# Exchanging real and imaginary rows in an S5 scan: by ScalarE and a second matrix product, or by transfers

## The chip, the core and the metric

The kernel runs on one core of a Trainium2 chip. The metric is device time in microseconds (us), from the start of the program to its end. The core has TensorE (PE in the rows; its weight loads are PEld), VectorE (DVE), ScalarE (ACT), GpSimd (POOL) and SyncE (SP), each of which works through its own instructions in the order in which they are written, and 16 DMA engines that move data between HBM (the device memory) and SBUF (the on-chip memory). Matrix products land in PSUM. SPq and ACTq are the parts of SyncE and ScalarE that issue transfers: a transfer that has to wait there for its source or its buffer holds up all that is queued behind it on that engine.

## The reference, cut to what matters

One inference step of a two-layer decoder, 2048 prompt tokens and 8 sample tokens, width 1024. Each layer projects its normed input and runs four head groups of width 256 side by side; the third of them (C) is S5, a diagonal complex state space model with 16 channel groups of 64 complex states. All of it is float32.

```python
proj = jnp.einsum('btd,de->bte', hn, w_in)      # 15 column groups, among them s_u and s_g
...
# _s5: u (B, T, 256) -> y, last state; x0 is the state before
bu_re = jnp.einsum('gpc,btgc->btgp', bb_re, ug)
bu_im = jnp.einsum('gpc,btgc->btgp', bb_im, ug)
def combine(e1, e2):
    a1r, a1i, b1r, b1i = e1
    a2r, a2i, b2r, b2i = e2
    return (a2r * a1r - a2i * a1i, a2r * a1i + a2i * a1r,
            a2r * b1r - a2i * b1i + b2r, a2r * b1i + a2i * b1r + b2i)
_, _, xr, xi = lax.associative_scan(combine, (A_re, A_im, bu_re, bu_im), axis=1)
y = jnp.einsum('gcp,btgp->btgc', c_re, xr) - jnp.einsum('gcp,btgp->btgc', c_im, xi)
...
mix = jnp.concatenate([ret_out, ml_out, s5_out, xa_out], axis=-1)
y = x + jnp.einsum('bte,ed->btd', mix, w_out)
```

## The kernel before

Each layer works through its prompt in four units of 512 tokens, so there are eight units. A unit is a row of weight groups of 256 columns (`m_v`, `s_u`, four `out` groups of the unit before, then `m_k` and so on to `r_g`); `group` multiplies each with the normed input `hT` or the mixed output `mix`. A weight arrives as `wraw`, ScalarE makes its high part `whi`, and VectorE and GpSimd make the low parts `wlo` (L338); three products of high and low parts stand for one exact one. Between two pieces of a group, `step_sides` moves every head group's generator on by one `yield`. That gives the program's order; a scheduler then lays out each engine's instructions, so a yield more or less shifts how much of the other groups' work stands between two steps.

S5 is the generator `s_core`. Four time steps are folded into one column, so a unit has 128 columns. The first 64 partitions hold real parts and the other 64 imaginary parts. The projected input goes to HBM as `ud` and comes back as X. Four times per unit (a quarter: four channel groups) there is a product of X with `Wi` into PSUM; a rotation by a table (`Cs`, `Sn`) that turns the complex decay into a real one; four real scans; the rotation back; and a product with `TW` that gives the output. A rotation needs each value's partner, the imaginary part beside the real one, which lies 64 partitions away. `swap` (L1267) fetches it by two transfers from SBUF to SBUF, 64 rows each: once ahead of the scans, from `V` into `Vs`, once after them, from `y` into `ys`. The program's own names are missing there: `t` in the rows is `V`, `y` or `t1`, and `sv` is `Vs` or `ys`. `xs` holds the rotated state, `xprev` the state that is carried on. The tables come from `s5_pre`, a generator that is run once per layer and writes them to HBM; `s_tables` loads them for each quarter.

The lines that the prediction speaks of: L1278 clears `xprev` at the start of a layer, L1282 loads X, L1289 is the product with `Wi`, L1294 and L1305 are the swaps, L1297 and L1309 the products that wait for them, L1302 the scans, L1310 GpSimd's product, L1311 the subtraction into `xs`, L1312 the copy into `xprev`, L1321 the product with `xs`. In the rows all matrix products stand as L180, transposes as L184, ScalarE's work as L187 and transfers as L190 or L193, since helpers write them; the rows' tile names tell them apart.

## Time and profile before

| | us |
|---|---|
| median of 3 runs | 2450.93 |
| lowest and highest | 2448.82, 2454.46 |
| the profiled execution | 2451.49 |
| its span, first to last instruction | 2449.7 |

| engine | busy us | share |
|---|---|---|
| TensorE, matmuls | 2175.0 | 89% |
| TensorE, weight loads (beside them) | 1989.2 | 81% |
| VectorE | 1663.0 | 68% |
| ScalarE | 978.3 | 40% |
| GpSimd | 845.2 | 35% |

The mean granted TensorE clock is 0.946 of full speed. The profile is of one execution. A row such as `L1309 DVE ... sv<-sv,sCS` gives the source line, the engine, the operation and what it writes and reads. A wait is named by what ended it, on the left the one that waited. The chain that ended last is followed back from the last instruction: at each step to what released it.

### The profile page before, as it was taken

Reading aid. Unit: us, or ns where it says so; the run is one execution under the profiler, and the core shown is the slowest. Engines: PE = TensorE matmul, PEld = TensorE weight load, DVE = VectorE, ACT = ScalarE, POOL = GpSimd, SP = SyncE. Lnnn points to the kernel's source line nnn. Section 1 sums busy time; section 2 is a strip of 40 time slices with the busy share of each in tenths; the row PEclk is TensorE's granted clock in tenths of the full one; section 3 lists DMA queues with packets and bytes.
Section 4 is the critical chain, followed back from the end, with each engine's and each line's share of the span. In section 5 each row is a group of like instructions: output and inputs, shape, how many; then the busy total and the mean of one; then the engine's idle time right before and its main releaser. Section 6 shows DMA issues by size and latency. Waiting matters only on the chain.

```text
span 2449.7 us, 44181 instructions
## 1 busy us (share of the span) xinstructions
PE 2175.0 (89%) x16130; PEld 1989.2 (81%) x16130; DVE 1663.0 (68%) x4003; ACT 978.3 (40%) x2152; POOL 845.2 (35%) x755
## 2 busy tenths in 40 slices
PE   7899957897889989987889999878989899999898
PEld 6788856897788878875888889777989787888788
DVE  7987835646675789773874767347576678868474
ACT  4554423342433544243442454223443354433343
POOL 2443312232233435442322343213332244434243
PEclk9999988899999999998999999888999999999899
DMA  7525374447374435735435442784446643573522
GB/s 222 168 86 179 99 109 96 132 137 94 88 208 130 127 115 171 217 99 102 121 110 178 118 132 77 171 183 87 87 101 208 198 125 113 161 247 121 101 64 105
DMA packets 355529, 329.78 MB, mean 135 GB/s; under 512 B 109144, under 2 KB 310040, under 8 KB 355312
## 3 DMA queue, kind: packets, MB, share of 16 engines
q1 hardware_dynamic: 329472, 266.53, 43.2%
q10 hardware_dynamic: 25840, 60.43, 7.8%
q8 instruction: 127, 2.08, 0.4%
q14 instruction: 90, 0.74, 0.1%
HBM read 265.40 MB, written 45.73 MB: 127 GB/s over the span
## 4 chain that ended last, share of the span: by engine, by line
PE 34%; DVE 15%; DMA 14%; issue 3%; ACT 2%; SPq 2%; POOL 1%; ACTq 0%; DVEq 0%; POOLq 0%
PE pm L180 24%; PE ps L180 8%; DMA sv<-t 4%; DMA wraw<-w_in 3%; PE ps L184 2%; DVE wlo L338 2%; SPq L190 2%; DVE sm L207 1%; DVE t L1302 1%; DMA X<-ud 1%; DMA s5im_p<-xprev 1%; DVE sm L206 1%; DVE sm L208 1%; DMA ud<-U 1%; DVE sv L1297 1%
## 5 line engine op out<-in xcount | busy, mean ns | idle before, releaser
L338 POOL TENSOR_TENSOR wlo<-wraw,whi 128x512 fp32r<-128x512 f32 (+1 forms) x280 | 400.5, 1435 | 655.9 <-ACT whi L187 513.7
L180 PE MATMUL pm<-hT,whi 128*128 128x512 f32 (+1 forms) x2240 | 610.1, 361 | 5.3 <-ACT whi L187 5.3
L180 PE MATMUL pm<-whi,hT 128*128 128x256 f32 (+1 forms) x3072 | 593.4, 289 | 16.3 <-ACT whi L187 13.7
L180 PEld LDWEIGHTS pm<-whi,hT 128*128 128x128 f32 x3072 | 488.8, 193 | 23.1 <-ACT whi L187 14.3
L187 ACT ACTIVATE whi<-wraw 128x512 fp32r<-128x512 f32 (+1 forms) x560 | 342.2, 629 | 392.1 <-PE pm L180 250.2
L180 PE MATMUL pm<-wlo,hT 128*128 128x256 f32 (+1 forms) x1536 | 440.8, 288 | 28.3 <-DVE wlo L338 27.1
L180 PEld LDWEIGHTS pm<-hT,whi 128*128 128x128 f32 x2240 | 397.4, 194 | 64.5 <-ACT whi L187 5.7
L180 PE MATMUL pm<-hT,wlo 128*128 128x512 f32 (+1 forms) x1120 | 398.0, 359 | 25.7 <-DVE wlo L338 24.3
L180 PE MATMUL pm<-whi,mix 128*128 128x256 f32 x2048 | 382.1, 286 | 9.1 <-ACT whi L187 5.5
L338 DVE TENSOR_TENSOR wlo<-wraw,whi 128x512 fp32r<-128x512 f32 (+1 forms) x280 | 248.7, 891 | 153.2 <-ACT whi L187 130.7
L180 PEld LDWEIGHTS pm<-whi,mix 128*128 128x128 f32 x2048 | 324.3, 193 | 11.3 <-ACT whi L187 5.8
L180 PEld LDWEIGHTS pm<-wlo,hT 128*128 128x128 f32 x1536 | 295.7, 193 | 31.6 <-DVE wlo L338 28.9
L180 PE MATMUL pm<-wlo,mix 128*128 128x256 f32 x1024 | 292.7, 287 | 8.8 <-DVE wlo L338 8.8
L180 PEld LDWEIGHTS pm<-hT,wlo 128*128 128x128 f32 x1120 | 215.7, 193 | 59.4 <-DVE wlo L338 26.6
L180 PEld LDWEIGHTS pm<-wlo,mix 128*128 128x128 f32 x1024 | 197.5, 193 | 10.1 <-DVE wlo L338 9.8
L1310 POOL TENSOR_TENSOR t<-t,sCS 128x512 f32<-128x512 f32 x32 | 45.7, 1427 | 216.5 <-DVE t L1302 66.7
L187 ACT ACTIVATE Pt<-ps,sm 128x256 f32<-128x256 f32 x128 | 58.9, 472 | 129.6 <-DVE sm L951 123.4
L1297 DVE TENSOR_TENSOR sv<-sv,sCS 128x512 f32<-128x512 f32 x32 | 25.0, 782 | 99.6 <-DMA sv<-t 99.6
L959 POOL TENSOR_TENSOR Pt<-Pt,sm 128x512 f32<-128x512 f32 x32 | 46.3, 1448 | 56.3 <-DVE sm L957 40.7
L207 DVE SCALAR_TENSOR_TENSOR sm<-sm,sm 128x8 f32<-128x8 f32 (+4 forms) x210 | 60.5, 290 | 3.5
L1309 DVE TENSOR_TENSOR sv<-sv,sCS 128x512 f32<-128x512 f32 x32 | 26.8, 838 | 51.1 <-DMA sv<-t 51.0
L1398 DVE TENSOR_TENSOR xr<-xr,pm 128x512 f32<-128x512 f32 x56 | 37.9, 678 | 31.2 <-PE pm L180 23.1
(442 smaller groups left out, 3717.5 us busy)
## 6 DMA issues: line engine op xcount, KB each, us to landing
wraw<-w_in SPq DMA_DIRECT2D x416, 256.0 KB
wraw<-w_out SPq DMA_DIRECT2D x128, 256.0 KB
sCS<-CS SPq DMA_DIRECT2D x32, 512.0 KB
sv<-t SPq DMA_DIRECT2D x128, 128.0 KB
xd<-xr SPq DMA_DIRECT2D x56, 256.0 KB
...
```

The costliest lines, as they stand in the source:

```text
L180: self.nc.tensor.matmul(out, lhsT, rhs, start=start, stop=stop, skip_group_check=skip)
L184: self.nc.tensor.transpose(out, in_, self.ident[:K, :K])
L187: self.nc.scalar.activation(out, in_, f, **kw)
L190: self.nc.sync.dma_start(out, in_)
L206: v.tensor_tensor(t, y, y, OP.mult)
L207: v.scalar_tensor_tensor(t, t, -0.5, b, op0=OP.mult, op1=OP.mult)
L338: e.tensor_tensor(lo[q][:, :, :n], r[q][:, :, :n], h.bitcast(F32), OP.subtract)
L959: e.tensor_tensor(Pt[:, 2 * x:2 * x + 2], Pt[:, 2 * x:2 * x + 2], sm_[:, 2 * x:2 * x + 2, None].to_broadcast([128, 2, MEM]), OP.mult)
L1297: v.tensor_tensor(Vs, Vs, Sn, OP.mult)
L1309: v.tensor_tensor(ys, ys, Sn, OP.mult)
L1310: gp.tensor_tensor(t1, y, Cs, OP.mult)
L1398: v.tensor_tensor(xr, xr, ps.rearrange("p (t c) -> p t c", t=2), OP.add)
```

## The change

The partner rows are no longer fetched by transfers. Ahead of the scans, ScalarE copies the product out of PSUM into `B` with the halves exchanged (two instructions of 64 rows), and VectorE reads the same PSUM for the other part. After the scans the partner isn't fetched at all: GpSimd writes y times `Cs` into `A`, VectorE writes y times `Sn` into `B`, both with their rows in place, and the sum that was `xs` is left to TensorE: `A` is multiplied with the table as before, and `B` with a third table, in which the two halves of the rows are exchanged. `B` stands one column later than `A`, whose first column is `xprev`, so the product with `B` has 127 columns. The carried state needs one column of the exchanged `B`, which ScalarE copies into `sh` in two instructions of 64 rows, and VectorE adds it to `A`'s last column.

Beside that: `xprev` is taken anew in each layer from a pool of two buffers; `s_core` has two more yields between the load of X and its first use, a quarter three instead of five, and one more after `yT`; `s5_pre` fetches `Bst` and `ct` ahead of where they are used, with three more yields; `TW` has a third part, which `s_tables` loads too; the pool `t2p` has a twelfth buffer.

```diff
@@ -135,7 +135,7 @@
         self.cp = e(tc.tile_pool(name="cp", bufs=1))
         self.wp = e(tc.tile_pool(name="wp", bufs=2))
         self.g4p = e(tc.tile_pool(name="g4p", bufs=16))
-        self.t2p = e(tc.tile_pool(name="t2p", bufs=11))
+        self.t2p = e(tc.tile_pool(name="t2p", bufs=12))
         self.t1p = e(tc.tile_pool(name="t1p", bufs=3))
         self.s64p = e(tc.tile_pool(name="s64p", bufs=12))
         self.smp = e(tc.tile_pool(name="smp", bufs=17))
@@ -255,7 +255,6 @@
         for t in self.Sr + self.Cm:
             nc.vector.memset(t, 0.0)
         self.mprev = c("mprev", [4, 8])
-        self.xprev = c("xprev", [128, SG])
         self.hS = [c(f"hS{i}", [128, 8, 40], F32R) for i in range(2)]
         for i in range(2):
             nc.vector.tensor_copy(self.hS[i].rearrange("p a b -> p (a b)"), zero)
@@ -269,7 +268,7 @@
         self.memd = []
         for l in range(self.depth):
             self.stab.append(dict(
-                Wi=self.dram([128, SG, 128], f"Wi{l}"), TW=self.dram([128, 2, 1024], f"TW{l}"),
+                Wi=self.dram([128, SG, 128], f"Wi{l}"), TW=self.dram([128, 3, 1024], f"TW{l}"),
                 CS=self.dram([128, 2, SG, 128], f"CS{l}"), Kd=self.dram([32, 16, 112], f"Kd{l}"), ab=self.dram([128, 3, SG], f"ab{l}"),
                 C1=self.dram([128, SG, SC], f"C1{l}")))
             self.memd.append((self.dram([128, 2, MEM], f"mk{l}"), self.dram([128, 2, GW], f"mv{l}")))
@@ -1078,6 +1077,13 @@
             self.dma(ar[64 * h:64 * h + 64], I["s5_a_re"][l].rearrange("g p -> p g"))
             self.dma(ai[64 * h:64 * h + 64], I["s5_a_im"][l].rearrange("g p -> p g"))
         self.dma(dt, AP(I["s5_log_dt"][l], 0, [[0, 128], [1, SG]]))
+        Bst = P1([2, SG, SC], "Bst")
+        for h in range(2):
+            for w in range(2):
+                src = I["s5_b_re" if h == w else "s5_b_im"][l]
+                self.dma(Bst[64 * h:64 * h + 64, w], src.rearrange("g p c -> p g c"))
+        yield
+        yield
         self.pexp(dt, SG)
         mag, th, cs, sn, k, tmp, thl = S(), S(), S(), S(), S(), S(), S()
         v.tensor_tensor(mag, ar, dt, OP.mult)
@@ -1141,13 +1147,17 @@
         sgn = self.smc[:, 0:1]
         fis = S()
         v.tensor_scalar(fis, fi, sgn, None, op0=OP.mult)
-        yield
-
-        Bst = P1([2, SG, SC], "Bst")
-        for h in range(2):
+        cts = []
+        for gh in range(2):
+            ct = P1([2, 128], "ct")
             for w in range(2):
-                src = I["s5_b_re" if h == w else "s5_b_im"][l]
-                self.dma(Bst[64 * h:64 * h + 64, w], src.rearrange("g p c -> p g c"))
+                src = I["s5_c_re" if w == 0 else "s5_c_im"][l].rearrange("g c p -> (g c) p")
+                s_ = src[gh * 128:(gh + 1) * 128, :]
+                self.dma(ct[:, 0, 64 * w:64 * w + 64], s_)
+                self.dma(ct[:, 1, 64 * (1 - w):64 * (1 - w) + 64], s_)
+            cts.append(ct)
+        yield
+
         Bb = P1([2, SG, SC], "Bb")
         bt = P1([SG, SC], "bt")
         bc = lambda x: x[:, :, None].to_broadcast([128, SG, SC])
@@ -1161,13 +1171,9 @@
         v.tensor_scalar(pims, pw[:, 1], sgn, None, op0=OP.mult)
 
         C1, C2 = packC[:, 0], packC[:, 1]
+        yield
         for gh in range(2):
-            ct = P1([2, 128], "ct")
-            for w in range(2):
-                src = I["s5_c_re" if w == 0 else "s5_c_im"][l].rearrange("g c p -> (g c) p")
-                s_ = src[gh * 128:(gh + 1) * 128, :]
-                self.dma(ct[:, 0, 64 * w:64 * w + 64], s_)
-                self.dma(ct[:, 1, 64 * (1 - w):64 * (1 - w) + 64], s_)
+            ct = cts[gh]
             ps = self.bank()
             self.tr(ps[:, 0:128], ct[:, 0, :])
             self.tr(ps[:, 128:256], ct[:, 1, :])
@@ -1231,6 +1237,9 @@
             v.tensor_tensor(W5, W5, w5, OP.subtract)
             self.dma(tab["TW"][:, 1, 256 * q:256 * q + 256].rearrange("p (g c) -> p g c", g=4),
                      W5[:, :, 1:5, :].rearrange("p g s c -> p g (s c)"))
+            for h in range(2):
+                self.dma(tab["TW"][64 * h:64 * h + 64, 2, 256 * q:256 * q + 256].rearrange("p (g c) -> p g c", g=4),
+                         W5[64 - 64 * h:128 - 64 * h, :, 1:5, :].rearrange("p g s c -> p g (s c)"))
             yield
             yield
 
@@ -1257,17 +1266,13 @@
     def s_tables(self, l, q):
         tab = self.stab[l]
         gs = slice(4 * q, 4 * q + 4)
-        TW, Wi = self.tb([128, 2, 256], "sTW", bufs=2), self.tb([128, 4, 128], "sWi")
+        TW, Wi = self.tb([128, 3, 256], "sTW", bufs=2), self.tb([128, 4, 128], "sWi")
         CS = self.tb([128, 2, 4, 128], "sCS")
         self.dma(Wi, tab["Wi"][:, gs])
         self.dma(CS.rearrange("p a g j -> p a (g j)"), tab["CS"][:, :, gs].rearrange("p a g j -> p a (g j)"))
         self.dma(TW, tab["TW"][:, :, 256 * q:256 * q + 256])
         return TW, Wi, CS[:, 0], CS[:, 1]
 
-    def swap(self, out, in_):
-        self.dma(out[0:64], in_[64:128])
-        self.dma(out[64:128], in_[0:64])
-
     def s_core(self, u, l, b):
         nc, v, gp = self.nc, self.nc.vector, self.nc.gpsimd
         while not self.pre_done[l]:
@@ -1275,51 +1280,56 @@
         if b == 0:
             self.abt = self.cp.tile([128, 3, SG], F32, name=self.nm("ab"), tag="ab", bufs=1)
             self.dma(self.abt, self.stab[l]["ab"])
+            self.xprev = self.cp.tile([128, SG], F32, name=self.nm("xprev"), tag="xprev", bufs=2)
             v.memset(self.xprev, 0.0)
         tb = self.s_tables(l, 0)
         X = self.g4([128, 8, 128], n="X")
         for s in range(4):
             self.dmaa(X[32 * s:32 * s + 32], AP(u["ud"], s * 128, [[512, 32], [32 * 512, 8], [1, 128]]))
         yield
+        yield
+        yield
         Y = self.g4([128, 8, 128], n="Y")
         for q in range(4):
             TW, Wi, Cs, Sn = tb
+            gq = slice(4 * q, 4 * q + 4)
             ps = self.bank()
             for g in range(4):
                 self.mm(ps[:, g * 128:(g + 1) * 128], Wi[:, g], X[:, 2 * q + g // 2], True, True)
             p3 = ps.rearrange("p (g j) -> p g j", g=4)
-            V, Vs, t1 = self.t2([128, 4, 128]), self.tb([128, 4, 128], "sv", bufs=2), self.t2([128, 4, 128])
-            self.act(V, p3)
+
+            B, t1, A = self.t2([128, 4, 128], n="sB"), self.t2([128, 4, 128], n="sy"), self.t2([128, 4, 129], n="sA")
             v.tensor_tensor(t1, p3, Cs, OP.mult)
-            self.swap(Vs, V)
-            yield
-            yield
-            v.tensor_tensor(Vs, Vs, Sn, OP.mult)
-            v.tensor_tensor(t1, t1, Vs, OP.add)
-            y = V
+            for h in range(2):
+                self.act(B[64 * h:64 * h + 64], p3[64 - 64 * h:128 - 64 * h])
+            v.tensor_copy(A[:, :, 0], self.xprev[:, gq])
+            v.tensor_tensor(B, B, Sn, OP.mult)
+            v.tensor_tensor(t1, t1, B, OP.add)
             for g in range(4):
                 gg = 4 * q + g
-                v.tensor_tensor_scan(y[:, g], self.abt[:, 2, gg:gg + 1].to_broadcast([128, 128]), t1[:, g],
+                v.tensor_tensor_scan(t1[:, g], self.abt[:, 2, gg:gg + 1].to_broadcast([128, 128]), t1[:, g],
                                      self.xprev[:, gg:gg + 1], OP.mult, OP.add)
-            ys = Vs
-            self.swap(ys, y)
-            yield
-            xs = self.t2([128, 4, 129], n="xs")
-            v.tensor_copy(xs[:, :, 0], self.xprev[:, 4 * q:4 * q + 4])
-            v.tensor_tensor(ys, ys, Sn, OP.mult)
-            gp.tensor_tensor(t1, y, Cs, OP.mult)
-            v.tensor_tensor(xs[:, :, 1:129], t1, ys, OP.subtract)
-            v.tensor_copy(self.xprev[:, 4 * q:4 * q + 4], xs[:, :, 128])
+
+            gp.tensor_tensor(A[:, :, 1:129], t1, Cs, OP.mult)
+            v.tensor_tensor(B, t1, Sn, OP.mult)
+            yield
+            sh = self.sm([128, 16])[:, :4]
+            for h in range(2):
+                self.act(sh[64 * h:64 * h + 64], B[64 - 64 * h:128 - 64 * h, :, 127])
             if q < 3:
                 tb = self.s_tables(l, q + 1)
             yield
+            v.tensor_tensor(self.xprev[:, gq], A[:, :, 128], sh, OP.add)
             yield
             po = self.bank()
             for a in range(2):
                 self.mm(po[:, a * 128:(a + 1) * 128], TW[:, 0, a * 128:(a + 1) * 128], X[:, 2 * q + a], a == 0, False, True)
-            for g in range(4):
-                self.mm(po[64 * (g % 2):64 * (g % 2) + 64, (g // 2) * 128:(g // 2 + 1) * 128],
-                        TW[:, 1, g * 64:(g + 1) * 64], xs[:, g, 0:128], False, g == 3, True)
+            for a in range(2):
+                for w, x, c0 in ((1, A, 0), (2, B, 1)):
+                    for e in range(2):
+                        g = 2 * a + e
+                        self.mm(po[64 * e:64 * e + 64, a * 128 + c0:(a + 1) * 128], TW[:, w, g * 64:(g + 1) * 64],
+                                x[:, g, 0:128 - c0], False, w == 2 and g == 3, True)
             self.act(Y[:, 2 * q:2 * q + 2].rearrange("p a j -> p (a j)"), po[:, :256])
         yd = self.dram([2, 8, SC, 4, 128], "yd")
         for g2 in range(2):
@@ -1330,6 +1340,7 @@
         yT = self.g4([128, 2, UT], n="yT")
         for gh in range(2):
             self.dmaa(yT[:, gh], AP(yd, gh * 128 * 512, [[512, 128], [1, 512]]))
+        yield
         yield
         if b == self.NU - 1:
             for h, on in enumerate(("s5re_p", "s5im_p")):
```

Three places show what this makes of the engines' order. The first is VectorE in the first quarter of the second unit of layer 1, before; `wlo` are weight splits, `xr` the output groups' sums.

```order
L1293 TENSOR_TENSOR t_3167_17640<-ps_17633,sCS_17556 128x512
L1308 COPY xs_17852<-xprev 128x4
L1398 TENSOR_TENSOR xr_17645<-xr_17645,pm_17647 128x512
L338 TENSOR_TENSOR wlo_17768<-wraw_17706,whi_17767 128x2x256
L1297 TENSOR_TENSOR sv_17639<-sv_17639,sCS_17556 128x512
L1298 TENSOR_TENSOR t_3167_17640<-t_3167_17640,sv_17639 128x512
L1302 SCALAR_TENSOR_TENSOR t_3165_17638<-ab_14390,xprev,t_3167_17640 128x128 x4
L1398 TENSOR_TENSOR xr_17714<-xr_17714,pm_17716 128x512
L1309 TENSOR_TENSOR sv_17639<-sv_17639,sCS_17556 128x512
L1311 TENSOR_TENSOR xs_17852<-t_3167_17640,sv_17639 128x4x128
L1312 COPY xprev<-xs_17852 128x4
```

And now. The work between the two products with `sCS` and the scans is one run, with the split of the next weights (`wlo`) behind the addition into `xprev`.

```order
L1302 TENSOR_TENSOR sy_17826<-ps_17820,sCS_17613 128x512
L1305 COPY sA_17827<-xprev_14525 128x4
L1306 TENSOR_TENSOR sB_17825<-sB_17825,sCS_17613 128x512
L1307 TENSOR_TENSOR sy_17826<-sy_17826,sB_17825 128x512
L1409 TENSOR_TENSOR xr_17758<-xr_17758,pm_17760 128x512
L1310 SCALAR_TENSOR_TENSOR sy_17826<-ab_14523,xprev_14525,sy_17826 128x128 x4
L1314 TENSOR_TENSOR sB_17825<-sy_17826,sCS_17613 128x512
L1322 TENSOR_TENSOR xprev_14525<-sA_17827,sm_17909 128x4
L337 TENSOR_TENSOR wlo_17894<-wraw_17754,whi_17893 128x2x256
```

What moved: the second and third step no longer wait for a transfer, the subtraction is gone, and the addition into `xprev` now reads `sA` of GpSimd and `sm` of ScalarE.

The second is TensorE at the end of the same quarter, where the products with the tables follow each other; `ps` is PSUM, `pm` the PSUM of the big products. Before:

```order
L180 MATMUL pm_17927<-whi_17840,mix_16938 128x256
L180 MATMUL ps_17994<-X_17560,sTW_17554 128x128 x2
L180 MATMUL ps_17994<-xs_17852,sTW_17554 64x128 x4
L180 MATMUL ps_18002<-X_17560,sWi_17859 128x128 x4
L180 MATMUL pm_18016<-whi_17917,mix_17151 128x256
```

And now:

```order
L180 MATMUL pm_17982<-whi_17897,mix_16995 128x256
L180 MATMUL ps_18049<-X_17617,sTW_17611 128x128 x2
L180 MATMUL ps_18049<-sA_17827,sTW_17611 64x128 x2
L180 MATMUL ps_18049<-sB_17825,sTW_17611 64x127 x2
L180 MATMUL ps_18049<-sA_17827,sTW_17611 64x128 x2
L180 MATMUL ps_18049<-sB_17825,sTW_17611 64x127 x2
L180 MATMUL ps_18061<-X_17617,sWi_17913 128x128 x4
L180 MATMUL pm_18083<-whi_17971,mix_17208 128x256
```

Four products of 64 rows of output by 127 columns came in. From the last product of `s_u` to the first product on X there stand 82 rows of TensorE before and 118 now in this unit, 156 and 174 in the last unit of layer 0, 76 and 168 in the last of layer 1. From the product on X in the second quarter of layer 1's first unit to that on `xs` there stand 186 rows before; to that on `sA` there stand 45 now, all of 512 columns.

The third is VectorE where layer 1 clears `xprev`. Before, ahead of a weight split in the last unit of layer 0:

```order
L705 TENSOR_TENSOR mh_11954<-mh_11954,sm_12772 128x512
L1231 TENSOR_TENSOR W_2294_12751<-W_2294_12751,w_2295_12752 128x320
L709 TENSOR_REDUCE sm_12778<-t_2298_12776 128x8
L1278 MEMSET xprev 128x16
L338 TENSOR_TENSOR wlo_12878<-wraw_12601,whi_12877 128x2x256
L202 TENSOR_SCALAR sm_12780<-sm_12778 128x8
```

Now both clears, one for each layer, stand among the first instructions of the program:

```order
L256 MEMSET Cm_156 128x260
L793 MEMSET mprev 4x8
L1284 MEMSET xprev_2859 128x16
L1284 MEMSET xprev_14525 128x16
L228 CAST identb<-ident 128x128
L385 TENSOR_TENSOR mT_196<-ps_198,mT_194 128x4x128
```

The clear of layer 1 went from the middle of the program to its start.

## Rows read from the trace of the kernel before

**Rows 1.** The page: busy us by engine; shares of the chain that ended last.
```profile
PE 2175.0 (89%) x16130; PEld 1989.2 (81%) x16130; DVE 1663.0 (68%) x4003; ACT 978.3 (40%) x2152; POOL 845.2 (35%) x755
...
PE 34%; DVE 15%; DMA 14%; issue 3%; ACT 2%; SPq 2%; POOL 1%; ACTq 0%; DVEq 0%; POOLq 0%
```

**Rows 2.** Waits of TensorE: who for whom, us in total, times, longest.
```profile
PE pm L180 <- DVE wlo L338: 60.5, 16, 18.0
PE pm L180 <- ACT whi L187: 26.2, 7, 11.1
PE ps L180 <- DVE xs L1311: 23.5, 4, 10.3
...
PE ps L180 <- DMA X<-ud: 17.1, 4, 10.6
...
PE ps L184 <- DMA ct<-s_c_im: 2.9, 2, 1.6
```

**Rows 3.** Waits of VectorE.
```profile
DVE sv L1297 <- DMA sv<-t: 99.6, 26, 15.1
DVE sv L1309 <- DMA sv<-t: 51.0, 17, 7.3
...
DVE wlo L338 <- DMA s5im_p<-xprev: 21.5, 1, 21.5
```

**Rows 4.** Timeline: start us, us, what, times, [idle before]; one quarter.
```profile
1624.76 0.85 DVE L1302 TENSOR_TENSOR_SCAN t<-ab,xprev,t 128x128 f32<-128x128 f32 x2
...
1625.64 1.10 SPq L190 DMA_DIRECT2D sv<-t  x2
...
1635.54 0.77 DVE L1309 TENSOR_TENSOR sv<-sv,sCS 128x512 f32<-128x512 f32 x1 [5.74 <-DMA sv<-t]
...
1637.16 1.12 PE L180 MATMUL ps<-xs,sTW 128*64 128x128 f32 x8 [10.26 <-DVE xs L1311]
```

**Rows 5.** Timeline where layer 1 clears xprev.
```profile
1108.94 0.62 ACT L187 ACTIVATE whi<-wraw 128x512 fp32r<-128x512 f32 x1
...
1129.20 0.69 DVE L338 TENSOR_TENSOR wlo<-wraw,whi 128x512 fp32r<-128x512 f32 x1 [21.48 <-DMA s5im_p<-xprev]
...
1129.95 0.79 PE L180 MATMUL pm<-hT,wlo 128*128 128x512 f32 x1 [18.04 <-DVE wlo L338]
```

**Rows 6.** Timeline, TensorE: first and last of eight idle times behind a swap.
```profile
267.49 0.87 PE L184 MATMUL ps<-ident,xt 128*128 128x128 f32 x3 [3.36 <-DVE mix L736]
...
2226.59 0.51 PE L180 MATMUL pm<-hT,wlo 128*128 128x512 f32 x1 [3.95 <-DVE wlo L338]
```

**Rows 7.** Stretches: us; busy of PE, PEld, DVE, ACT, POOL; granted clock; DMA share, GB/s.
```profile
325.00:405.00 80.00, 48.46 (x323) 44.08 (x324) 31.58 (x60) 18.07 (x39) 13.51 (x12) 0.74 0.65 99
...
1040.00:1135.00 95.00, 69.00 (x481) 60.38 (x480) 58.09 (x150) 31.51 (x79) 32.01 (x35) 0.84 0.48 86
...
1600.00:1670.00 70.00, 48.11 (x363) 46.05 (x362) 32.79 (x101) 18.00 (x46) 10.11 (x8) 0.80 0.79 162
```

**Rows 8.** Groups by line and shape: busy us, mean ns | idle before us.
```profile
L180 PE MATMUL pm<-hT,whi 128*128 128x512 f32 x1344 | 437.7, 407 | 5.3 <-ACT whi L187 5.3
...
L180 PE MATMUL ps<-xs,sTW 128*64 128x128 f32 x256 | 22.9, 304 | 23.5 <-DVE xs L1311 23.5
...
L1309 DVE TENSOR_TENSOR sv<-sv,sCS 128x512 f32<-128x512 f32 x32 | 26.8, 838 | 51.1 <-DMA sv<-t 51.0
L1311 DVE TENSOR_TENSOR xs<-t,sv 128x512 f32<-128x512 f32 x32 | 25.6, 801 | 0.8
...
L187 ACT ACTIVATE aq<-pm 64x512 fp32r<-64x512 f32 x24 | 14.0, 590 | 24.1 <-PE pm L180 17.6 <-DVE aq L572 6.3
...
L187 ACT ACTIVATE sm<-sm 128x16 f32<-128x16 f32 x12 | 2.6, 214 | 17.9 <-DVE sm L754 16.6 <-DVE sm L1062 1.0 <-DVE sm L1065 0.2
...
L1310 POOL TENSOR_TENSOR t<-t,sCS 128x512 f32<-128x512 f32 x32 | 45.7, 1427 | 216.5 <-DVE t L1302 66.7 <-issue 37.5 <-DVE RT L819 24.1
```

**Rows 9.** The tile sv: ns min/median/max of L1309, first and last start, shape.
```profile
L1309 DVE TENSOR_TENSOR sv<-sv,sCS x32: 672/692/1773, 225.5 to 2263.3; 128x512 f32<-128x512 f32 x32
```

2 lines of the change are left out of this document (1 added, 1 removed).

## The prediction

> **What bounds the kernel now.** I read the page's engine shares first. TensorE is busy 89% of a span of 2449.7 us and no other engine passes 68%, so the time is TensorE's 2175 us plus what holds it up; the chain that ended last has 14% in DMA and 15% in VectorE beside 34% in TensorE [rows 1]. So I asked next what TensorE waits for: low parts of the weights made by VectorE (60.5 us in 16 waits), high parts made by ScalarE (26.2), the S5 product on `xs` (23.5 in 4), and the first S5 product on X (17.1 in 4) [rows 2]. VectorE stands behind most of that, and its own longest DMA waits are the swap: 99.6 us ahead of L1297 and 51.0 ahead of L1309, together 150.6, and once 21.5 us for the output transfer of `xprev` [rows 3]. VectorE works in the order written, so while it waits for a swap, every weight split behind it waits too.
>
> One quarter of S5 shows the pattern. The last scans run until about 1625.6, the swap is issued at 1625.64, and VectorE goes on at 1635.54: 9.9 us for a transfer whose result is used at once. TensorE then ends an idle time of 10.26 us at 1637.16, on `xs` [rows 4]. Elsewhere the swap holds something else up. I followed each longer idle time of TensorE back by its releasers: beside the 23.5 us on `xs`, eight end in a VectorE instruction that stood behind a swap (or behind a table load that a swap's buffer held back), from 3.36 us at 267.49 to 3.95 us at 2226.59, with six between; they sum to 35.7 us [rows 6]. All that TensorE loses to the swap is thus 59.2 us, 39% of the 150.6 us that VectorE loses.
>
> **What goes, part by part.** The sum is made against the profiled execution, 2451.5 us with 1.8 us outside its span; the median of the three runs is 2450.9, so nothing has to be shifted.
>
> *xprev.* Before, layer 1 clears the one `xprev` after its output transfer has landed: VectorE stands 21.48 us, and TensorE 18.04 us, until 1129.95 [rows 5]. With two buffers the order has both clears among VectorE's first instructions. What is late next? The high part that this split needs left ScalarE at 1109.6 [rows 5], so nothing: **-18.0 us**.
>
> *X.* The two added yields put TensorE rows between the last `s_u` product and the first product on X. By the order these are 82 before and 118 now in the unit at 1549, 156 and 174 in the one at 970, 76 and 168 in the last. The waits were 17.1 us in all, the longest 10.6 [rows 2]; A row of 512 columns takes 0.33 us (437.7/1344) [rows 8] and I count half for one of 256, so 36 more rows cover 6 to 12 us. I leave 4.6 us standing: **-12.5 us** (bounds -7 and -17.1).
>
> *Tables.* Parameters for `Bst` and `ct` are fetched two yields earlier: the wait on `ct`, **-2.9 us** [rows 2].
>
> *The swap.* Its 128 transfers are gone from SyncE, and 59.2 us of TensorE's idle time ended in them. Not all of it comes back. In eight of the twelve cases TensorE waited for other work behind the swap, and that work then meets what else was late: weight loads, ScalarE, the other branches. Fewer yields also bring the product on `sA` and `sB` nearer to its inputs. Ends: 0, if everything had another wait underneath, and -59.2. I take two thirds, nearer to the full sum because the xprev case shows work ready and only blocked: **-39.5 us**.
>
> *Clock.* After such idle times the granted clock is at the lower level (1.2 GHz) for a while. In the stretch 325 to 405 the mean is 0.74, so 41.6 of its 80 us were at half clock; TensorE was idle 31.5 us of the stretch, so at least 10.1 us of work ran at half speed. Stretch 1040 to 1135 gives 30.4 less 26.0, and 1600 to 1670 gives 28.0 less 21.9 [rows 7]. Sum 20.6 us of work at half speed: **-10.3 us**.
>
> **What comes.** *Second product.* 128 matmuls of the shape of the one on `xs`, whose 128 take 22.9 us of TensorE [rows 8]. Nothing hides it, since TensorE is the bound: **+22.9 us**. Its weight loads lie beside the matmuls.
>
> *ScalarE.* One evacuation of 512 columns becomes two, of 64 rows each, 590 ns apiece by the same shape for `aq`, and two of four columns come on top, 0.2 us each by the smallest near them, 214 ns for 16 columns [rows 8]: about 1.0 us a quarter, 32 us in all, on an engine that is busy 40% [rows 1]. It counts only where TensorE waits for a split of ScalarE, 26.2 us [rows 2]; bounds 0 and 10, **+3 us**, since 32 us is a thirtieth of its work.
>
> *VectorE.* It loses the subtraction of L1311, 32 of 801 ns or 25.6 us [rows 8]; the other counts stay. I book nothing for it. It has a new wait: the addition into `xprev` (L1322) stands right behind the product on `sB` and waits for GpSimd's `sA`, with a weight split queued behind it on VectorE and TensorE waiting for that split. GpSimd takes 1.43 us there and VectorE's product 0.84, the mean of L1309's group [rows 8]; 0.6 us if GpSimd is free, about 2 us if another such operation is ahead. Before, the subtraction waited for the same engine and lost 0.8 us in all. Ends 0 and 64 us of VectorE; I take 0.9 us a quarter, 29 us, and by the ratio of 39% above **+11 us**.
>
> L1309 itself is usually undisturbed: minimum 672, median 692, longest 1773 ns [rows 9]. In the Trainium skill, GPSIMD Engine Reference, section 1 Specifications, a rule speaks against the new form: GpSimd shares SBUF interfaces with VectorE and contends with VectorE instructions of two SBUF inputs, and now the two products start off the same scan together. Were every one as long as the longest, the row's numbers would give 32 x 1.08 = 35 us of VectorE, or some 14 us on TensorE, and the sum would be 2419; the median speaks for a small part of it.
>
> *At nothing:* `sTW` loads grow from 256 to 384 KB, 4 MB in all where 17 MB of swaps go; the third table is written by eight small transfers per layer; the tables are ready three steps later, but the order still has S5 of the first unit of each layer end earlier than before.
>
> **Sum.** 2451.5 - 18.0 - 12.5 - 2.9 - 39.5 - 10.3 + 22.9 + 3 + 11 = 2405 us, 1.9% less.
>
> **The rivals.** *All of it comes back* (0.18). Every swap wait (59.2) and X wait (17.1) is gone, and VectorE's shorter queue pays for its new wait and for ScalarE: 2451.5 - 18 - 17.1 - 2.9 - 59.2 - 10.3 + 22.9 = 2367. For it: VectorE stood 150 us. Against: the second longest sum of waits, for low parts, is partly at unit ends, where norm arithmetic fills VectorE.
>
> *The swap was hidden* (0.18). Only xprev, X, tables and the clock behind xprev (2.2) count, with the product and ScalarE against them: 2451.5 - 18 - 12.5 - 2.9 - 2.2 + 22.9 + 3 = 2442. For it: only four of twelve waits end in `xs` itself. Against: the 9.9 us of rows 4. By the Trainium skill, DMA: Bandwidth & Descriptors, section Anatomy of one DMA, a transfer costs about 2.0 us plus its bytes at 436 GB/s, an estimate of 2.3 us for this one (the section speaks of another issuing path); by that the exchange through ScalarE would save little and this rival would hold. The trace disagrees, 9.9 us in rows 4.
>
> *The new chain is longer than its cover* (0.14), the one that ends slower. With yields removed, TensorE comes to `sA` and `sB` sooner. In the second quarter of layer 1's first unit 45 rows of 512 columns stand between, 186 rows of all kinds before. The chain without queueing is two evacuations, two products and sums of about 0.8, four scans of 1.7 together, twice the 0.85 of two [rows 4], and GpSimd: 1.2 + 1.6 + 1.7 + 1.4 = 5.9 us; the cover is 45 x 0.33 = 14.7 us [rows 8]. Queues would have to add 9 us there, on VectorE behind L1322 and on GpSimd behind weight splits. It decides once a quarter costs TensorE 1.45 us more than booked (46.3/32); at 2.5 us the time is 2405 + 80 = 2485. Against: VectorE has no DMA in this chain any more.
>
> **Numbers.** The forecast has 0.50, within 2385 to 2430. Leaving out the slower rival and the outer edges, the range is 2352 to 2450. A measurement here tells about 0.2% (5 us) from no change. Faster: 0.50 + 0.18 + 0.13 of the hidden case = 0.81; within 0.2%: its rest, 0.05; slower: 0.14.
>
> **What would show it.** Right: no wait of TensorE on `ps<-X,sWi` over 5 us; VectorE's largest DMA wait is far below 99.6; no 18 us hole where layer 1 clears `xprev`; products on `sB` at about 23 us; mean clock above 0.946. Wrong: waits of TensorE on `sA` or `sB` that sum to over 46 us; VectorE waiting long at L1322; TensorE's idle total not below 275 us (2449.7 less 2175.0); or, since a scheduler laid out all engines anew, new holes at places that this change doesn't touch, which no row here can price.

## The result

| | median, us | range, us | runs | ratio to before, 95% interval |
|---|---|---|---|---|
| before | 2449.88 | 2440.67 to 2454.46 | 4 | |
| after | 2368.9 | 2363.64 to 2380.36 | 4 | 0.968, 0.9635 to 0.9726 |

The change is faster by 3.2%, 81 us. The forecast was 2405, so it had the sign right, and the time lies inside its range, but 36 us below it. The profiled execution of after took 2380.36 us, its span is 2378.5, and it is the longest of the four.

First the page of after: busy us of each engine, and the shares of the chain that ended last; then its view by core, with the mean granted clock.

```profile
PE 2179.9 (92%) x16385; PEld 2002.2 (84%) x16386; DVE 1655.3 (70%) x3971; ACT 1014.2 (43%) x2252; POOL 862.0 (36%) x755
...
PE 38%; DVE 8%; DMA 7%; issue 4%; POOL 1%; ACT 1%; SPq 0%; ACTq 0%; DVEq 0%; POOLq 0%
```

```profile
core 0: 2378.5 us, clock 0.959
```

Against [rows 1] TensorE's busy time rose by 4.9 us while the span fell by 71.2, so the span without TensorE fell from 274.7 to 198.6 us. The shares of the two chains can't be set side by side: those of before add up to 71% of the span, those of after to 59%. In a run that differs in one buffer and takes the same time (eleven `t2p` buffers, below) they add up to 93%, with 18% for VectorE and 13% for the DMAs, so no smaller share of either is shown.

Then the waits of TensorE in after (who for whom: us in total, times, longest).

```profile
PE pm L180 <- DVE wlo L337: 28.0, 12, 8.2
PE ps L184 <- DVE xt L355: 23.3, 7, 8.0
PE pm L180 <- ACT whi L187: 21.7, 11, 8.0
PE ps L180 <- ACT inter L187: 12.2, 2, 10.4
PE ps L180 <- DMA X<-ud: 11.1, 2, 8.4
...
PE ps L180 <- DMA sWi<-Wi: 9.2, 2, 6.7
...
PE ps L180 <- ACT sB L187: 6.2, 3, 3.0
```

The wait for low parts fell from 60.5 to 28.0, and that on X from 17.1 only to 11.1 [rows 2]. The one on `xs` (23.5) has no successor: the products on `sA` and `sB` wait for nothing. The 6.2 us of the last row belong to another product, of `mqT` and `mkT`, which starts when ScalarE's copy of S5's first product out of PSUM has ended (at 732.66, 1873.44 and 2140.96). Some rows grew: that on `xt`, the input of transposes (5.2 before), that on `inter`, and that on `sWi`, a table's load, which had no row before.

The waits of VectorE in after, the same columns:

```profile
DVE wlo L337 <- ACT whi L187: 119.1, 73, 9.8
DVE sy L1302 <- PE ps L180: 48.0, 15, 9.4
...
DVE sy L1302 <- DMA sCS<-CS: 21.9, 3, 10.5
DVE sB L1306 <- ACT sB L187: 21.6, 21, 4.1
...
DVE xprev L1322 <- ACT sm L187: 11.2, 7, 8.0
...
DVE xprev L1322 <- POOL sA L1313: 7.0, 7, 1.2
```

The 150.6 us of the swaps [rows 3] are gone. In their place VectorE waits 48.0 us for the first product, 21.6 for the exchange and 18.2 at L1322, in many short waits.

One quarter in after, from VectorE's timeline (start us, us, what, times), as [rows 4] show one of before:

```profile
1547.36 0.69 DVE L1307 TENSOR_TENSOR sy<-sy,sB 128x512 f32<-128x512 f32 x1
1548.09 1.61 DVE L1310 TENSOR_TENSOR_SCAN sy<-ab,xprev,sy 128x128 f32<-128x128 f32 x4
1549.73 0.69 DVE L1314 TENSOR_TENSOR sB<-sy,sCS 128x512 f32<-128x512 f32 x1
...
1552.12 0.69 DVE L337 TENSOR_TENSOR wlo<-wraw,whi 128x512 fp32r<-128x512 f32 x1
...
1552.80 0.16 DVE L1322 TENSOR_TENSOR xprev<-sA,sm 128x4 f32<-128x4 f32 x1
```

From the last scan to the product with `Sn` it was 9.9 us; now one follows the other at 1549.73, and a weight split gets through between L1314 and L1322.

The groups that the change added or altered (busy us, mean ns | idle before):

```profile
L1313 POOL TENSOR_TENSOR sA<-sy,sCS 128x512 f32<-128x512 f32 x32 | 57.7, 1805 | 186.8 <-DVE sy L1310 118.6 <-PE ps L180 16.3 <-DVE sm L203 14.3
L187 ACT ACTIVATE sB<-ps 64x512 f32<-64x512 f32 x64 | 37.9, 592 | 126.3 <-DVE sy L1302 96.3 <-DMA sp<-sd 9.8 <-issue 9.6
...
L180 PE MATMUL ps<-sA,sTW 128*64 128x128 f32 x256 | 29.1, 292 | 0.0
L1314 DVE TENSOR_TENSOR sB<-sy,sCS 128x512 f32<-128x512 f32 x32 | 26.9, 839 | 0.4
...
L180 PE MATMUL ps<-sB,sTW 128*64 128x127 f32 x256 | 26.8, 279 | 0.0
```

### The profile page after: what moved, and what is told of

It is laid out like the page before. It is cut to its first block, busy times and chain, and to the rows that moved or that the text cites. A ratio compares the mean times of both kernels' runs of the same rounds, so it can differ in the third digit from the quotient of the medians.

```text
span 2378.5 us, 44503 instructions
## 1 busy us (share of the span) xinstructions
PE 2179.9 (92%) x16385; PEld 2002.2 (84%) x16386; DVE 1655.3 (70%) x3971; ACT 1014.2 (43%) x2252; POOL 862.0 (36%) x755
## 4 chain that ended last, share of the span: by engine, by line
PE 38%; DVE 8%; DMA 7%; issue 4%; POOL 1%; ACT 1%; SPq 0%; ACTq 0%; DVEq 0%; POOLq 0%
PE pm L180 27%; PE ps L180 9%; PE ps L184 2%; DVE wlo L337 1%; DMA wraw<-w_in 1%; DMA xd<-xr 1%; DVE sm L206 1%; DVE sm L207 1%; DMA y_prompt<-fx 1%; DVE sm L208 1%; DMA sCS<-CS 1%; DMA xt<-xd 1%; DMA sWi<-Wi 0%; DVE sy L1310 0%; SPq L190 0%
## 5 line engine op out<-in xcount | busy, mean ns | idle before, releaser
L337 POOL TENSOR_TENSOR wlo<-wraw,whi 128x512 fp32r<-128x512 f32 (+1 forms) x280 | 410.4, 1473 | 666.3 <-ACT whi L187 578.8
L180 PE MATMUL pm<-hT,whi 128*128 128x512 f32 (+1 forms) x2240 | 598.7, 355 | 1.4 <-ACT mkT L187 1.0
L180 PEld LDWEIGHTS pm<-whi,hT 128*128 128x128 f32 x3072 | 496.5, 195 | 28.0 <-ACT whi L187 15.3
L180 PEld LDWEIGHTS pm<-hT,whi 128*128 128x128 f32 x2240 | 390.3, 191 | 58.5 <-issue 1.5
L337 DVE TENSOR_TENSOR wlo<-wraw,whi 128x512 fp32r<-128x512 f32 (+1 forms) x280 | 260.1, 931 | 123.8 <-ACT whi L187 119.1
L1313 POOL TENSOR_TENSOR sA<-sy,sCS 128x512 f32<-128x512 f32 x32 | 57.7, 1805 | 186.8 <-DVE sy L1310 118.6
L187 ACT ACTIVATE sB<-ps 64x512 f32<-64x512 f32 x64 | 37.9, 592 | 126.3 <-DVE sy L1302 96.3
L1302 DVE TENSOR_TENSOR sy<-ps,sCS 128x512 f32<-128x512 f32 x32 | 22.0, 687 | 69.9 <-PE ps L180 48.0
L184 PE MATMUL ps<-ident,xt 128*128 128x128 f32 x256 | 41.9, 316 | 31.1 <-DVE xt L355 23.3
L206 DVE TENSOR_TENSOR sm<-sm 128x8 f32<-128x8 f32 (+4 forms) x210 | 66.0, 316 | 3.9
```

The costliest lines, as they stand in the source:

```text
L180: self.nc.tensor.matmul(out, lhsT, rhs, start=start, stop=stop, skip_group_check=skip)
L184: self.nc.tensor.transpose(out, in_, self.ident[:K, :K])
L187: self.nc.scalar.activation(out, in_, f, **kw)
L206: v.tensor_tensor(t, y, y, OP.mult)
L337: e.tensor_tensor(lo[q][:, :, :n], r[q][:, :, :n], h.bitcast(F32), OP.subtract)
L1302: v.tensor_tensor(t1, p3, Cs, OP.mult)
```

## The experiments

Each kernel was compared with the kernel before on the same chip. So that they can be set beside each other, the table gives each ratio times 2450 us, with its 95% interval; the text below gives medians as well.

| kernel | runs | at 2450 us |
|---|---|---|
| after | 4 | 2372 (2361 to 2383) |
| before without both swaps | 4 | 2361 (2356 to 2366) |
| before without the first | 4 | 2405 (2395 to 2414) |
| before without the second | 4 | 2421 (2414 to 2428) |
| before with two `xprev` | 10 | 2444 (2440 to 2449) |
| after without the product on `sB` | 4 | 2352 (2347 to 2357) |
| after with one `xprev` | 4 | 2385 (2380 to 2389) |
| after, eleven `t2p` buffers | 4 | 2370 (2363 to 2378) |
| the same with unread transfers, 128 KB each | 4 | 2404 (2397 to 2411) |
| the same with unread transfers, 4 KB each | 4 | 2393 (2384 to 2401) |
| after with one yield behind the load of X | 4 | 2395 (2387 to 2402) |
| after without the wait at L1322 | 4 | 2382 (2375 to 2388) |
| after, three edits more | 4 | 2350 (2341 to 2359) |

### What the swaps cost

In the kernel before, each product reads the rows in place.

```diff
-            self.swap(Vs, V)
...
-            v.tensor_tensor(Vs, Vs, Sn, OP.mult)
+            v.tensor_tensor(Vs, V, Sn, OP.mult)
...
-            self.swap(ys, y)
...
-            v.tensor_tensor(ys, ys, Sn, OP.mult)
+            v.tensor_tensor(ys, y, Sn, OP.mult)
```

> The kernel before without the two swaps per quarter: the product that waited for the swapped rows reads the unswapped ones (V and y), so the exchange is left out and the S5 numbers are not the reference's; yields, xprev and products are as before. Theory (VectorE blocked by the transfers is what costs): most of the 59.2 us of TensorE's idle time behind swaps comes back with some of the clock, 2450 - 40 - 10 = 2400, between 2370 and 2410. Rival (the swap was hidden, other waits lie underneath): 2440 or more. A gain near the whole change's 81 us would say that xprev, X and yields add little.

Measured: 2360.05 us, less than the 2370 to 2410 that were expected. That is 89 us at 2450 where the forecast had booked 49.8 for swap and clock. The rival that the swap was hidden is out. The lines of its page, of TensorE's waits and of ScalarE's:

```profile
PE 2161.2 (92%) x16128; PEld 1984.6 (84%) x16130; DVE 1662.6 (71%) x4003; ACT 980.1 (42%) x2152; POOL 873.5 (37%) x755
```

```profile
PE pm L180 <- DVE wlo L338: 30.3, 13, 9.9
```

```profile
ACT whi L187 <- DMA wraw<-w_in: 41.2, 15, 9.6
```

TensorE's work is 13.8 us shorter than in [rows 1] with the same products, which goes with the clock (0.946 before, 0.958 here; two pages of such kernels at one clock, before and before with two `xprev`, differ by 6.4). The rest of its span of 2355.4 fell by 80.5 us. Some 7 of these aren't the swap's: layer 1's clear of `xprev` still waits for the output transfer here, but TensorE loses 11.10 us behind it (until 1097.92) and not 18.04. The chains followed in the trace of before had found 59.2. What they may have missed is what the transfers do to the other queues. These are rows of the kernel before, waits of ScalarE and of SyncE's queue:

```profile
ACT whi L187 <- DMA wraw<-w_in: 67.7, 24, 10.4
```

```profile
SPq L190 <- DMA sv<-t: 31.2, 8, 8.1
SPq L190 <- DVE t L1302: 29.7, 14, 6.3
...
SPq L190 <- ACT t L187: 14.6, 8, 3.8
```

In the last three rows SyncE stood 75.5 us for a swap or for what a swap reads, with weight loads queued behind, and ScalarE waited 67.7 us for those loads where it waits 41.2 without the swaps. But the 75.5 us are no measure of the loss: without the swaps SyncE's waits for VectorE and GpSimd to be done with a low part rise from 488.0 to 556.6 us, so a queue that gets there earlier mostly waits for a free buffer. Nor did TensorE's own wait for high parts fall (26.2 and 29.3); what fell is its waits for VectorE, for low parts by 30.2 with the `xprev` hole among them, for `xs` by 23.5 and for `E` by some 17. How much of the 89 us went through the queue isn't shown by these rows. SyncE's queue before, then without the swaps:

```profile
SPq L190 <- DVE wlo L338: 383.2, 111, 18.3
SPq L190 <- POOL wlo L338: 104.8, 90, 8.1
```

```profile
SPq L190 <- DVE wlo L338: 425.6, 124, 19.7
SPq L190 <- POOL wlo L338: 131.0, 107, 8.1
```

The two swaps one at a time, each the matching half of the diff above:

> The kernel before without the first swap of each quarter, ahead of the scans (the product reads V unswapped; that exchange is left out). Theory (cost goes with VectorE's waits, 99.6 of 150.6 us): two thirds of the 90 us of b_noswap, 2450 - 60 = 2390. Rival (the second swap, on which the product of TensorE waits, carries most): 2425 or more.

> The kernel before without the second swap of each quarter, after the scans (the product reads y unswapped; that exchange is left out). Theory (51.0 of 150.6 us): one third of 90 us, 2450 - 31 = 2420. Rival: 2395 or less. If neither b_no1 nor b_no2 gains its share, one swap alone keeps most of the wait.

Measured: 2399.94 and 2419.31 us, at 2450 a gain of 45 and of 29, in the order of the 99.6 and 51.0 of VectorE's waits in [rows 3]; together 74 of the 89. The intervals of some 10 and 7 us leave the ratio of the two open.

### What a transfer costs that nobody waits for

After with eleven `t2p` buffers, and four transfers per quarter as the swaps issued them, into a tile that nothing reads; its control has the eleven buffers alone.

```diff
-        self.t2p = e(tc.tile_pool(name="t2p", bufs=12))
+        self.t2p = e(tc.tile_pool(name="t2p", bufs=11))
...
+        self.idle = c("idle", [128, 4, 128])
...
+            for h in range(2):
+                self.dma(self.idle[64 * h:64 * h + 64], self.Dt[64 - 64 * h:128 - 64 * h].rearrange("p a b c -> p (a b) c"))
             v.tensor_copy(A[:, :, 0], self.xprev[:, gq])
...
+            for h in range(2):
+                self.dma(self.idle[64 * h:64 * h + 64], self.Dt[64 - 64 * h:128 - 64 * h].rearrange("p a b c -> p (a b) c"))
             sh = self.sm([128, 16])[:, :4]
```

> The changed kernel with four transfers of 64 x 512 a quarter put back on SyncE at the places of the old swaps, from a constant into a tile that nobody reads (t2p at 11 buffers, to make room). The traffic and SyncE's slots of the swaps are back, and nobody waits for them. Theory (VectorE's waiting was the cost): within 8 us of a_t211. Rival (the traffic, or weight loads queued behind the swaps on SyncE): 27 us or more above a_t211.

> The changed kernel with 11 buffers in t2p instead of 12: the control for a_idle4, and a measure of what an edit that moves no work does through the scheduler. Theory: within 8 us of 2369. Rival (the twelfth buffer carries part of the gain): 2380 or more.

Measured: 2402.1 us, and 2370.09 for the control, so the twelfth buffer does nothing that can be told and the unread transfers cost 32 us. Is it their bytes or their places in SyncE's queue? The same with tiles of 4 instead of 128 columns a group:

```diff
-        self.idle = c("idle", [128, 4, 128])
+        self.idle = c("idle", [128, 4, 4])
...
-                self.dma(self.idle[...], self.Dt[...].rearrange("p a b c -> p (a b) c"))
+                self.dma(self.idle[...], self.Dt[...].rearrange("p a b c -> p (a b) c")[:, :, 0:4])
```

> The kernel after, with eleven t2p buffers and with four transfers per quarter on SyncE that nobody reads, as in the run with idle transfers of 128x512 (2402 us, against 2370 for eleven buffers alone), but each is of 64x16 elements, 4 KB instead of 128 KB. Same number and same places of issue, a thirty-second of the bytes. If those 32 us came from the bytes that share the DMA engines with the weight loads: 2370 to 2377. If they came from the slots in SyncE's queue (the issue, and the wait for the earlier transfer into the same tile, with weight loads behind): 2395 to 2405. Half and half: about 2386.

Measured: 2390.01 us, 20 above the control; at 2450 it is 23, and 34 for the large ones. So about two thirds of the cost come without the bytes, though the intervals leave that share open between a third and all. The rows of SyncE's queue, first with the large transfers, then with the small:

```profile
SPq L190 <- DMA idle<-Dt: 69.1, 59, 4.2
```

```profile
SPq L190 <- DMA idle<-Dt: 43.4, 47, 3.0
```

Even a transfer of 4 KB holds the queue up, since the next into the same tile waits for it. The pages say where it ends: against the control TensorE's time outside its work is 14.8 us longer with the large transfers (204.3 and 189.5) and 12.1 with the small (201.6), and its work 13.9 and 4.4 longer. So the places in the queue cost idle time, and the bytes seem to show in TensorE's work, at a granted clock of 0.952 where the small have 0.960. That is a hint from single executions, beside pages that differ by 6.4 at one clock, and why bytes would do that stays open.

### The second product

```diff
-                for w, x, c0 in ((1, A, 0), (2, B, 1)):
+                for w, x, c0 in ((1, A, 0),):
...
-                                x[:, g, 0:128 - c0], False, w == 2 and g == 3, True)
+                                x[:, g, 0:128 - c0], False, g == 3, True)
```

> The changed kernel without the product on sB: that half of the output sum is left out. Theory (TensorE is the bound, nothing hides the product): 2369 - 23 = 2346 by the rows of before; by the rows of after (29.1 + 26.8 for sA and sB against 22.9) up to 2336. Rival (it lies in TensorE's idle time): 2364 or more.

Measured: 2350.72 us, 18 less than after, 20 at 2450, with about 12 of uncertainty from the two intervals. The booked 22.9 agrees. So does TensorE's busy time on its page, 21.5 us less than the 2179.9 of after:

```profile
PE 2158.4 (92%) x16129; PEld 1982.6 (85%) x16130; DVE 1651.1 (70%) x3971; ACT 1016.2 (43%) x2252; POOL 861.1 (37%) x755
```

### The state's buffer

One part of the change alone, in the kernel before:

```diff
-        self.xprev = c("xprev", [128, SG])
...
+            self.xprev = self.cp.tile([128, SG], F32, name=self.nm("xprev"), tag="xprev", bufs=2)
```

> The kernel before with xprev taken anew in each layer from two buffers, and nothing else. Theory: the 18.0 us hole at 1130 goes, with 2 us of clock: 2450 - 20 = 2430. Rival (another late operand or a new order fills the hole): within 5 us of 2450.

Measured: 2444.22 us, a gain of 6 and not 18. The hole of [rows 5] has only moved. The timelines of SyncE's queue, ScalarE and TensorE there (in brackets the idle time before):

```profile
1105.98 0.70 SPq L190 DMA_DIRECT2D s5im_p<-xprev  x1
...
1107.51 4.37 SPq L190 DMA_DIRECT2D wraw<-w_in  x4
...
1128.33 0.63 ACT L187 ACTIVATE whi<-wraw 128x512 fp32r<-128x512 f32 x1 [12.62 <-DMA wraw<-w_in]
...
1129.41 1.87 PE L180 MATMUL ps<-suT,sWi 32*128 32x8 f32 x8 [10.79 <-ACT cso L187]
```

The first weight load issued from 1107.51 on, behind the output transfers of `xprev` and a table's write, lands at about 1128, hardly sooner than that output did in before (1129.20). ScalarE waits 12.62 us for it, its next instruction is the copy `cso`, and TensorE stands 10.79 us. In before these four loads are issued at 1129.92 only, when VectorE is past the clear.

And taken away from the kernel after:

```diff
-            self.xprev = self.cp.tile([128, SG], F32, name=self.nm("xprev"), tag="xprev", bufs=2)
+            self.xprev = self.cp.tile([128, SG], F32, name=self.nm("xprev"), tag="xprev", bufs=1)
```

> The changed kernel with one buffer for xprev. Theory: the clear of layer 1 waits again for the output transfer with weight splits behind it: 2369 + 18 to 20 = 2388. Rival (in the new order the clear stands where nothing needed is behind it, since S5 ends earlier in the unit): within 5 us of 2369.

Measured: 2383.9 us, 15 more than after. VectorE and TensorE in its timeline:

```profile
1035.91 0.07 DVE L1284 MEMSET xprev<- 128x16 f32 x1 [10.50 <-DMA s5im_p<-xprev]
...
1038.52 0.80 PE L180 MATMUL pm<-hT,wlo 128*128 128x512 f32 x1 [7.48 <-DVE wlo L337]
```

The clear waits again and TensorE loses 7.48 us behind it; in after TensorE has no idle time above 2 us between 1020 and 1045. The buffer reads as worth more in after (13 to 15 us) than alone in before, but with some 12 us of uncertainty on the first the two aren't told apart.

### The yields behind the load of X

```diff
             self.dmaa(X[32 * s:32 * s + 32], AP(u["ud"], s * 128, [[512, 32], [32 * 512, 8], [1, 128]]))
         yield
-        yield
-        yield
```

> The kernel after with one yield instead of three between the load of X and its first use. Theory of the prediction: the two yields save 12.5 us of waiting for X, so without them about 2381 and the wait of TensorE on X goes back from 11.1 toward 17 us and more. Rival, by the trace of the kernel after, where that wait only fell from 17.1 to 11.1 us: 2372 to 2376. A second rival: the yields put S5's chain later against the rest, and without them the time is the same or less, 2362 to 2371.

Measured: 2393.07 us, 24 more than after, outside all that was expected. TensorE's waits there, then three places of its timeline, two of TensorE and one of ScalarE:

```profile
PE ps L180 <- DVE E L860: 16.5, 3, 14.5
PE ps L180 <- DMA X<-ud: 15.6, 3, 10.3
```

```profile
1494.65 1.62 PE L180 MATMUL ps<-X,sWi 128*128 128x128 f32 x6 [10.35 <-DMA X<-ud]
...
1597.90 0.63 ACT L187 ACTIVATE gl<-yT 128x512 f32<-128x512 f32 x1 [8.79 <-DMA yT<-yd]
...
1599.65 0.69 PE L180 MATMUL ps<-mv,E 128*128 128x65 f32 x2 [14.46 <-DVE E L860]
```

In sum the wait on X makes only 4.5 us of it (15.6 against 11.1). But the 15.6 us stand in the three units that the prediction counted (2.89, 10.35 and 2.33 us, at 921.99, 1494.65 and 2059.11), and in after these units have 2.71 us left, at 1500.29. There the yields saved 12.9 us. The other 8.4 us of after are new, in a unit that waits for X neither here nor in before:

```profile
348.73 2.04 PE L180 MATMUL ps<-X,sWi 128*128 128x128 f32 x8 [8.37 <-DMA X<-ud]
```

The second hole ends in another head group's `E` on VectorE, which stands in the order behind an instruction on `gl`; `gl` is S5's output on its way through the gelu, and ScalarE had waited 8.79 us for it to come back from HBM as `yT`. It is not the missing yields' alone, since after has a hole near the same place:

```profile
1601.56 0.81 ACTq L193 DMA_DIRECT2D yT<-yd  x2
1602.42 0.60 ACT L187 ACTIVATE mo<-pm 128x512 f32<-128x512 f32 x1 [20.49 <-DMA wraw<-w_in]
...
1603.89 0.43 PE L180 MATMUL ps<-whi,hS 128*40 128x256 f32 x1 [10.36 <-ACT inter L187]
```

ScalarE does nothing there for 20 us but issue the load of `yT`, which reads what SyncE's last four writes `yd` (issued from 1591.45 on) put into HBM; `mo` and `inter` stand behind it, and TensorE waits for `inter`. The row names a weight load; that the load of `yT` held ScalarE up is read from the order. That hole is the longest of after, and the missing yields add 4.1 us to it. So the yields are worth more than booked: about half of it lies at X, 12.9 of some 24 us, and where the rest lies was not traced to an end.

### The wait at L1322

```diff
-            sh = self.sm([128, 16])[:, :4]
-            for h in range(2):
-                self.act(sh[64 * h:64 * h + 64], B[64 - 64 * h:128 - 64 * h, :, 127])
...
-            v.tensor_tensor(self.xprev[:, gq], A[:, :, 128], sh, OP.add)
+            v.tensor_copy(self.xprev[:, gq], t1[:, :, 127])
```

> The kernel after without the wait at L1322: the carried state is taken from the scan's own last column, so VectorE waits there for neither GpSimd nor ScalarE, and ScalarE's two copies of four columns are gone. What it leaves out is the rotation back of the carried state. The prediction booked 11 us for this wait and 0.4 of 1.0 us of ScalarE's work per quarter (1.2 of its 3 us): 2357 by that. Scaled by the 19.6 us of waiting before L1322 that the trace of the kernel after shows, at the prediction's 39%: 2361. Rival, that other work was late there too and the wait costs nothing: 2366 to 2372.

Measured: 2377.8 us, not less than after; the two can't be told apart. VectorE's 18.2 us there cost TensorE nothing that can be measured, unless the new order of the other work took back what the wait gave.

### A version with three edits more

```diff
-        TW, Wi = self.tb([128, 3, 256], "sTW", bufs=2), self.tb([128, 4, 128], "sWi")
+        TW, Wi = self.tb([128, 3, 256], "sTW", bufs=2), self.tb([128, 4, 128], "sWi", bufs=2)
...
+            ps = self.bank()
+            self.tr(ps[:SG, 0:128], self.xprev)
+            so = self.t1([128, 128], n="sxo")
+            self.act(so[:SG], ps[:SG, 0:128])
             for h, on in enumerate(("s5re_p", "s5im_p")):
-                self.dma(self.O[on][l, 0].rearrange("g p -> p g"), self.xprev[64 * h:64 * h + 64])
+                self.dma(self.O[on][l, 0], so[:SG, 64 * h:64 * h + 64])
```

> A version meant to beat both: the kernel after with eleven t2p buffers, two buffers for the table Wi (whose loads TensorE waits 9.2 us for after the change), and the last state transposed by TensorE and written as rows of 256 bytes instead of elements of 4 bytes. If the scattered output transfer still holds up the weight loads queued behind it, and Wi's second buffer ends its wait: 2352 to 2362. If two xprev buffers already hide all of it: 2366 to 2372.

Measured: 2347.56 us (2338.83 to 2360.76), ratio 0.9591 (0.9555 to 0.9628): 21 us less than after, less than was expected, and faster than both. Its page, and a row of TensorE's waits:

```profile
PE 2166.9 (93%) x16388; PEld 1990.9 (85%) x16388; DVE 1655.2 (71%) x3971; ACT 1014.0 (43%) x2254; POOL 863.3 (37%) x755
```

```profile
PE pm L180 <- DVE wlo L337: 17.4, 9, 4.2
```

The diff leaves out the eleven `t2p` buffers and the same second buffer of `sWi` for the sample tokens. In its span of 2337.0 us 170.1 lie outside TensorE's work, where after has 198.6 and after with eleven buffers 189.5; the profiled execution is the fastest of the four here and the longest in after, so the second difference is the fairer one. TensorE's wait for `sWi`, 9.2 us in after but 2.7 with eleven buffers, is gone. Which of the two edits, table or output, brings how much wasn't run apart.

## Why the prediction was right, point by point

| term | booked, us | measured, us |
|---|---|---|
| swap and clock | -39.5 and -10.3 | -89, some 7 of it at the clear of `xprev` |
| of it TensorE's work, by the clock | -10.3 | -13.8, by the two pages |
| `xprev` | -18.0 | -6 alone, -13 to -15 in after |
| X | -12.5 | -23 or -24, of it 12.9 in the units meant, less 8.4 of a new wait |
| `ct` | -2.9 | not run apart |
| second product | +22.9 | +18 to +20 |
| new wait at L1322, with ScalarE's small copies | +11, and 1.2 of the 3 | nothing that can be told |
| ScalarE's copies of halves | 1.8 of the 3 | not run apart |

The measured terms don't add up: with -14 for `xprev` and the booked -2.9 for `ct` they give about -109 us, and the whole change gave -78 at 2450. The measured time also lies outside the 2385 to 2430 that the prediction gave its forecast; it lies in the stated range through the share of the first rival.

**The step that was mis-sized is the swap.** The mechanism was right: VectorE stood for a transfer whose result was used at once, and TensorE behind it. But the prediction took "two thirds" of a sum of 59.2 us, because in eight of twelve cases other work "then meets what else was late: weight loads, ScalarE". It took these as independent of the swap. The run without swaps gave back 89 us, some 7 of them at the clear of `xprev`. The 82 left are more than the full 59.2 with the clock's 10.3, so the third that was held back as waiting underneath was not there. That the swap made the rest late itself, through SyncE's queue, is one account: ScalarE waited 26.5 us less for weight loads without it, and a chain from TensorE's idle time back through VectorE doesn't show such a thing. Unread transfers of the same number and size cost 32 us in the kernel after; 89 less 7 and 32 is 50, as much as was booked for the waiting and the clock. That subtraction crosses two kernels, and each figure is uncertain by 5 to 10 us, so it is an account that fits, not a proof. The other account, that the eight idle times followed back were too few of those that the swap caused, fits the rows on `E` as well and was not parted from it.

**xprev: "so nothing" was wrong.** The high part for that one split was ready, but in the run with two `xprev` the next weight load wasn't, since it was queued behind the same output transfer. The rows of before couldn't show its landing, as it was issued there only after the hole; that it would be next in the queue was there to see.

**X was right where it was counted, and half of the whole.** The 12.9 us at the three units agree with the 12.5 booked. The prediction said no wait on X over 5 us; one of 8.4 stands in another unit, the second of layer 0, at 348.7, for which it had counted no rows. The other half of what the yields are worth lies elsewhere, and it had no term.

**The product and the new wait.** The product's price, taken from the group of the same shape [rows 8], holds. Its groups read 29.1 and 26.8 us against 22.9 for `xs`, 33 more, but TensorE's busy time in after with and without the second product is 2179.9 and 2158.4, only 21.5 more: busy times of neighbouring groups overlap. L1322 was booked at the ratio that TensorE lost to the swap, 39%, and that ratio didn't carry over: the waits there sum to 18.2 us in 14, one of 8.0 among them.

**GpSimd.** The Trainium skill, GPSIMD Engine Reference, section 1 Specifications, has GpSimd and VectorE contend for shared SBUF interfaces. Here the trace agrees on one side alone: GpSimd's product went from 1427 ns [rows 8] to 1805, and VectorE's beside it stayed at 838 and 839. In the quarter shown above VectorE's product starts at 1549.73 and GpSimd's 0.05 us later, to last 1.80 us; three that ran in before with VectorE idle beside them took 1.28 to 1.29. The 35 us of VectorE that the prediction weighed by the longest row did not come.

**What was to be seen.** No 18 us hole, the clock above 0.946 (0.959), TensorE's time outside its work below 275 us (198.6) and no sum of 46 us on `sA` and `sB` came as said, and VectorE's largest DMA wait is 21.9; the products on `sB` read 26.8 instead of about 23, and a wait on X over 5 us is there. The new hole of which it warned came too, 10.36 us at 1603.89, though not quite at a place that the change leaves alone: it stands at S5's own load of `yT`.

**The rivals.** *All of it comes back* gave 2367 and lies nearest to 2368.9. Its two claims, that every swap wait returns and that VectorE's shorter queue pays for the new wait, are what the runs without swaps and without L1322's wait show; its claim that X's wait is gone is not. What spoke against it there, waits for low parts at unit ends, was called the second longest sum, but is the longest [rows 2]; it fell by half. That it is so near is in part luck: it reached the time with 69.5 us for swap and clock where 89 were measured. *The swap was hidden* fell by that run. The rule weighed there, about 2.0 us plus the bytes at 436 GB/s (the Trainium skill, DMA: Bandwidth & Descriptors, section Anatomy of one DMA), gives the 2.3 us estimated there; the trace has 9.9 in [rows 4]. *The new chain is longer than its cover* fell by the trace: in after TensorE waits for neither `sA` nor `sB`, with eleven buffers 3.8 us for `sA`, and 8.1 with one yield behind the load of X, far from 46.

**What stays open.** Without swaps and without any exchange the kernel takes 2361; after without its second product takes 2352, though it also has the gains on `xprev`, X and `ct`, some 40 us. About 30 us, uncertain by 20, are thus either paid for the exchange itself (ScalarE's halves, fewer yields in a quarter, larger tables), or the gains aren't additive, since each shortens idle time that another would have covered. Neither is shown. The new wait on `sWi` would speak for the first, but with eleven buffers it is 2.7 us at the same time of the whole, and what the version with three edits got back can't be put down to it. A kernel after with the first swap put back, to part them, wasn't tried.
